# Strassen-Winograd products for gate and up, and a down stage of its own, in a hybrid decoder layer

## The chip, the cores and the metric

The kernel runs on one core of one Trainium2 chip. The metric is the device time of one execution in microseconds. The names of the engines are those of the profile: PE is TensorE (PEld its weight loads), DVE VectorE, ACT ScalarE, POOL GpSimd and SP the queue that issues most DMAs.

## What is computed

One decoder layer over T = 1032 tokens (1024 of a prompt and 8 single new tokens), model width D = 1024, feed-forward width 2816:

```python
h = x + 0.5 * swiglu(rmsnorm(x, g_ff1), w_ff1_gate, w_ff1_up, w_ff1_down)
z = rmsnorm(h, g_mix) @ w_in              # latents of MLA, and q, k, v, o, gates of mLSTM
...                                       # attention (8 heads), mLSTM (4 heads), caches
h = h + concat(rmsnorm(a), headnorm(m)) @ w_out
h = h + 0.5 * swiglu(rmsnorm(h, g_ff2), w_ff2_gate, w_ff2_up, w_ff2_down)
h = h + sigmoid(rmsnorm(h, g_ple) @ w_ple_gate) * (pe @ w_ple_proj)
y = rmsnorm(h, g_final)
# swiglu(x, wg, wu, wd) = (silu(x @ wg) * (x @ wu)) @ wd
```

## The kernel before

Activations lie feature-major: 8 tiles of 128 features by 1032 tokens, and the tokens are worked on in three groups of N = 344. Every large product is done with each operand split in two fp32r parts, hi and lo, and three matmuls, hi·hi, hi·lo and lo·hi (`mm3`, L198 to L200). `split` (L180, L184) makes the parts: ScalarE casts hi, and VectorE (or GpSimd, L182) subtracts it.

`ffn` runs both feed-forward blocks. Its unit is one block of 128 of the 2816 hidden features (there are 22, called f) for one token group: 24 matmuls for gate into the bank pg, 24 for up into pu, then silu, the product with up (L355), and the split into the tiles hd, which stay in SBUF. f is taken in blocks of 5, 5, 5, 5 and 2. After each block `down` multiplies its hidden features with the down weight into pd and adds half of it to h (L367). In the last block units and downs of the groups alternate (`halves`, `close`), so that the next norm can start (`nxt.a` sums squares, `nxt.b` scales and splits).

The first FFN starts on tokens that are not normalised yet (`lift`, L295): its gate and up banks are multiplied by the norm's factor r afterwards (L349, L351). The second one uses `n2`, whose groups are normalised during the output projection.

`ple_proj` computes the projection of the per-layer embedding, 8 row tiles × 3 groups of 6 matmuls (bank pj), stored to the DRAM tensor ppd. It is a generator: `em.add(ple_proj(), PP_E, PP_D)` hands it to the emitter, which puts a unit of it between the instructions of the attention each time a number of estimated microseconds has been spent. The attention's other tiles: pss scores (L1166), pT transposes (L1198), po products with v (L1221), and for the new tokens ss (L1074) and ol, whose cached keys kt and nt GpSimd gathers (L1051, L1060).

TensorE and SP run in the order in which the program issues their instructions; ScalarE, VectorE and GpSimd are ordered by the scheduler.

## Time and profile before

| what | value |
|---|---|
| median of 3 runs | 2342.53 us (2341.18 to 2345.26) |
| the profiled execution, its own time | 2340.3 us |
| its span in the trace | 2338.5 us |
| mean granted clock of TensorE | 0.989 |
| matmuls | 14,543 |
| DMA | 167.28 MB, 72 GB/s on the mean |

The span runs from the first to the last recorded instruction; 1.8 us of the execution lie around it. Busy times of the engines overlap, so they are read against the span one by one. A matmul's recorded duration overlaps its neighbours' too; the distance between starts is what a stream of them costs.

### The profile page before, as it was taken

How to read it: one execution, taken by the hardware profiler on the slowest of the kernel's cores; microseconds unless marked ns; L12 is line 12 of the kernel's file. 1: busy time of each engine (PE TensorE's matmuls, PEld its weight loads, DVE VectorE, ACT ScalarE, POOL GpSimd, SP SyncE). 2: the span in 40 equal slices, each digit the busy share in tenths (PEclk: the TensorE clock that was granted, in tenths of full speed). 3: DMA queues.
4: the chain of work that ended last, by engine and by line, in shares of the span. 5: the costliest groups of instructions: out<-in, count | busy, mean ns of one | idle time of the engine just before them, and what ended most of it. 6: DMA issues, size and time to landing. Idle time of an engine off the chain costs nothing.

```text
span 2338.5 us, 35223 instructions
## 1 busy us (share of the span) xinstructions
PE 2288.4 (98%) x14543; PEld 2178.7 (93%) x14543; DVE 1046.3 (45%) x2147; ACT 708.7 (30%) x1448; POOL 410.4 (18%) x397
## 2 busy tenths in 40 slices
PE   8999999999999899999999999999999999999997
PEld 8999999999999799999756579999999999999996
DVE  7332232332334747446656677423223223223575
ACT  5211211211212433434555553321120210211353
POOL 4100101101102421112376325100000000000243
PEclk9999999999999999999999999999999999999998
DMA  3111112011021322223755531101112112112113
GB/s 136 39 53 55 30 53 64 25 56 55 28 68 55 137 34 94 83 74 127 198 154 150 161 109 37 46 27 56 55 32 73 32 38 72 37 34 81 58 39 107
DMA packets 73752, 167.28 MB, mean 72 GB/s; under 512 B 10656, under 2 KB 36864, under 8 KB 73592
## 3 DMA queue, kind: packets, MB, share of 16 engines
q1 hardware_dynamic: 63304, 142.69, 19.6%
q0 software_dynamic: 6832, 18.12, 3.0%
q10 hardware_dynamic: 3456, 4.23, 0.6%
q8 instruction: 114, 1.87, 0.3%
q14 instruction: 46, 0.38, 0.1%
HBM read 141.33 MB, written 23.65 MB: 71 GB/s over the span
## 4 chain that ended last, share of the span: by engine, by line
PE 89%; DVE 6%; ACT 2%; DMA 1%; issue 1%; POOL 0%; SPq 0%; DVEq 0%; ACTq 0%; POOLq 0%
PE pd L199 7%; PE pd L200 7%; PE pd L198 7%; PE pg L200 7%; PE pu L199 7%; PE pu L198 7%; PE pu L200 7%; PE pg L199 7%; PE pg L198 7%; PE pz L199 3%; PE pz L198 3%; PE pz L200 3%; PE pss L1166 3%; DVE xf L281 2%; PE po L1221 2%; PE pT L1198 2%
## 5 line engine op out<-in xcount | busy, mean ns | idle before, releaser
L198 PE MATMUL pd<-hdh,wh 128*128 128x344 f32 x1056 | 340.6, 323 | 5.9 <-ACT hdh L180 5.9
L199 PE MATMUL pd<-hdl,wh 128*128 128x344 f32 x1056 | 339.6, 322 | 3.4 <-DVE hdl L184 3.3
L199 PE MATMUL pg<-xn,wh 128*128 128x344 f32 x1056 | 338.7, 321 | 2.8 <-DVE xn L184 1.9
L198 PE MATMUL pg<-xn,wh 128*128 128x344 f32 x1056 | 338.3, 320 | 1.7 <-ACT xn L180 1.3
L200 PE MATMUL pd<-hdh,wl 128*128 128x344 f32 x1056 | 339.1, 321 | 0.0
L198 PE MATMUL pu<-xn,wh 128*128 128x344 f32 x1056 | 338.7, 321 | 0.3 <-DVE si L349 0.3
L200 PE MATMUL pg<-xn,wl 128*128 128x344 f32 x1056 | 338.4, 320 | 0.5 <-DVE wl L184 0.4
L199 PE MATMUL pu<-xn,wh 128*128 128x344 f32 x1056 | 338.1, 320 | 0.0
L200 PE MATMUL pu<-xn,wl 128*128 128x344 f32 x1056 | 338.0, 320 | 0.0
L180 ACT CAST wh<-wr 128x1024 fp32r<-128x1024 f32 (+2 forms) x195 | 180.4, 935 | 371.7 <-PE pd L199 304.6
L184 DVE TENSOR_TENSOR wl<-wr,wh 128x1024 fp32r<-128x1024 f32 (+2 forms) x195 | 216.0, 1108 | 115.4 <-ACT wh L180 110.3
L355 DVE TENSOR_TENSOR hp<-si,pu 128x344 f32<-128x344 f32 x132 | 67.6, 512 | 420.6 <-PE pu L200 413.1
L367 DVE SCALAR_TENSOR_TENSOR h<-pd,h 128x344 f32<-128x344 f32 x240 | 122.9, 514 | 281.3 <-PE pd L200 281.3
L256 POOL TENSOR_TENSOR sq<-sq,sq 128x344 f32<-128x344 f32 x66 | 70.0, 1060 | 798.5 <-ACT sq L251 771.2
L198 PEld LDWEIGHTS pd<-hdh,wh 128*128 128x128 f32 x1056 | 199.9, 189 | 7.1 <-ACT hdh L180 6.7
L199 PEld LDWEIGHTS pd<-hdl,wh 128*128 128x128 f32 x1056 | 199.9, 189 | 4.6 <-DVE hdl L184 4.2
L199 PEld LDWEIGHTS pg<-xn,wh 128*128 128x128 f32 x1056 | 199.0, 188 | 4.2 <-DVE xn L184 3.1
L198 PEld LDWEIGHTS pg<-xn,wh 128*128 128x128 f32 x1056 | 199.0, 188 | 2.4 <-ACT xn L180 1.6
L200 PEld LDWEIGHTS pg<-xn,wl 128*128 128x128 f32 x1056 | 199.0, 188 | 1.1 <-DVE wl L184 1.1
L200 PEld LDWEIGHTS pd<-hdh,wl 128*128 128x128 f32 x1056 | 200.0, 189 | 0.0
L198 PEld LDWEIGHTS pu<-xn,wh 128*128 128x128 f32 x1056 | 199.0, 188 | 1.0 <-issue 0.8
L199 PEld LDWEIGHTS pu<-xn,wh 128*128 128x128 f32 x1056 | 199.0, 188 | 0.2
(374 smaller groups left out, 3974.9 us busy)
## 6 DMA issues: line engine op xcount, KB each, us to landing
wr<-in_wu SPq DMA_DIRECT2D x44, 512.0 KB, 3.6
wr<-in_wg SPq DMA_DIRECT2D x43, 512.0 KB, 3.7
wr<-in_wd SPq DMA_DIRECT2D x64, 320.0 KB, 2.9
wr<-in_w_in SPq DMA_DIRECT2D x22, 512.0 KB, 6.2
h<-in_xT SPq DMA_DIRECT2D x24, 172.0 KB, 4.3
hsp<-h SPq DMA_DIRECT2D x8, 516.0 KB, 2.6
ppd<-pj SPq DMA_DIRECT2D x24, 172.0 KB, 3.3
h<-hsp SPq DMA_DIRECT2D x8, 516.0 KB, 3.9
```

The costliest lines, as they stand in the source:

```text
L180: act.copy(hi, src)
L184: dve.tensor_tensor(out=lo, in0=src, in1=hi.bitcast(F32), op=ALU.subtract)
L198: pe.matmul(ps, whi, xhi, start=first, stop=False)
L199: pe.matmul(ps, whi, xlo, start=False, stop=False)
L200: pe.matmul(ps, wlo, xhi, start=False, stop=last)
L256: pool.tensor_tensor(out=acc[0], in0=acc[0], in1=q, op=ALU.add)
L281: dve.scalar_tensor_tensor(out=x, in0=s[:, c], scalar=gc[:, g0 + k:g0 + k + 1], in1=r, op0=ALU.mult, op1=ALU.mult)
L355: dve.tensor_tensor(out=p, in0=s, in1=pu, op=ALU.mult)
L367: dve.scalar_tensor_tensor(out=h[m][:, c], in0=pd, scalar=0.5, in1=h[m][:, c], op0=ALU.mult, op1=ALU.add)
L1166: pe.matmul(ps[:, 0:n], qp[:, qs], kp[0:96, kc], start=True, stop=True)
L1198: pe.transpose(ps[:, PV_POS[j], :], P[j][:, kb * 128:(kb + 1) * 128], ident)
L1221: pe.matmul(po[64 * i:64 * i + 64, p0 * 128:256], v, px[:, 2 * i + p0:2 * i + 2, :].rearrange("p j q -> p (j q)"), start=kb == 0, stop=kb ...
```

## The change

- **Gate and up.** Tokens are cut in quarters of QN = 258; two quarters form a half of HC = 516. For each half and each of gate and up, a pair of f (256 hidden features), the model width's two halves and two quarters of tokens make a 2 × 2 by 2 × 2 block product. It is done with seven block products for eight (Winograd's form). `operands` makes the eight token operands once per FFN: the four blocks b11, b21, b12, b22 of the normalised tokens, and four differences t1 to t4, all split. `weights` loads a pair's 2 × 512 KB and builds the weight operands with four 512-column sums, and splits. `chain(i)` runs the products b11, b21, t2, t1, t3, t4, b22, each 12 matmuls of 258 columns for each half, with copies c1, u2 and u3 out of the banks. The first pair of each FFN is done with all eight products (`plain`).
- **Hidden features.** silu(gate) · up is stored by GpSimd's DMA queue in DRAM (hidd), unsplit.
- **Down** is a stage behind all gate and up products, in five passes: halves mh of the output features and token groups, (0, g0 and g1), (0, g2), (1, g0), (1, g1), (1, g2), each over all 22 f in PSUM. Hidden blocks of three f are read back (hr) and split, the down weight is read in a new layout once per half, and the residual h is read back, from the input or from a spill hsp2.
- **Start.** The embedding's projection runs at the start of the program, in two parts around the sums of squares. The first FFN's tokens are loaded as rows xr and normalised before the products; lift and the later scaling are gone.
- **Second FFN.** Its norm's factors r2 and first operands are built during the output projection (BUILD_AT).

```diff
-FBLOCKS = [5, 5, 5, 5, 2]
+QN = T // 4
...
+AHEAD_D = 5
...
+AH_IN = {(3, 12): (0,), (4, 4): (1,), (4, 12): (2,)}
+PL_A, PL_B = 13, 5
+BUILD_AT = (2, 4, 5, 6)
...
+    def operands(at, rr, g0, hf, x):
...
+        for n, kh, j in (("b11", 0, 0), ("b21", 1, 0), ("b12", 0, 1), ("b22", 1, 1)):
+            q = 2 * hf + j
+            t = raw[n] = B([128, 4, QN], F32, "xf")
+            for k in range(4):
+                kk = 4 * kh + k
+                dve.scalar_tensor_tensor(out=t[:, k, :], in0=at(kk, q), scalar=gc[:, g0 + kk:g0 + kk + 1], in1=rr[:, QS[q]], op0=ALU.mult, op1=ALU.mult)
+            put(n, t)
+            yield
+        t = None
+        for n, a, b in (("t1", "b12", "b11"), ("t3", "b22", "b12"), ("t2", "b22", "b11"), ("t4", "b21", "b22")):
+            o = "b22" if n == "t2" else "b21" if n == "t4" else b
+            dve.tensor_tensor(out=raw[o], in0=raw[a], in1=raw[b], op=ALU.subtract)
+            put(n, raw[o])
...
+    def weights(ap, j, plain):
...
+            put(("b11", "b21"), r1)
+            s1 = B([128, 512], F32, "ws")
+            dve.tensor_tensor(out=s1, in0=a21, in1=a22, op=ALU.add)
+            dve.tensor_tensor(out=a21, in0=a11, in1=a21, op=ALU.subtract)
+            dve.tensor_tensor(out=a11, in0=s1, in1=a11, op=ALU.subtract)
+            dve.tensor_tensor(out=a12, in0=a12, in1=a11, op=ALU.subtract)
+            yield
+            put(("t2", "b22"), r1)
...
+        def store(i, hf, o):
+            pool.dma_start(out=hidd[i - 1:i + 1, :, hf * HC:(hf + 1) * HC].rearrange("a p c -> p a c"),
+                           in_=o.rearrange("p (a q) n -> p a (q n)", a=2))
...
+        def chain(i):
...
+            for hf in product(b1, "b11", True, True):
+                o[hf] = B([128, 4, QN], F32, "hp" if up else "gs")
+                c1[hf] = SC(QN, p="c1")
+                act.copy(c1[hf], b1[hf])
...
+            for hf in product(b2, "b21", True, True):
+                dve.tensor_tensor(out=o[hf][:, 0], in0=b2[hf], in1=c1[hf], op=ALU.add)
...
+            for hf in product(b1, "t2", False, True):
+                u2[hf] = SC(QN, p="u2")
+                act.copy(u2[hf], b1[hf])
...
+            for hf in product(b3, "t1", True, True):
+                pass
+            for hf in product(b1, "t3", False, True):
+                u3[hf] = SC(QN, p="u3")
+                act.copy(u3[hf], b1[hf])
+                dve.tensor_tensor(out=o[hf][:, 3], in0=b3[hf], in1=u3[hf], op=ALU.add)
...
+            for hf in product(b1, "t4", False, True):
+                if up:
+                    dve.tensor_tensor(out=o[hf][:, 2], in0=b1[hf], in1=gs[hf][:, 2], op=ALU.mult)
...
+            for hf in product(b3, "b22", False, True):
+                dve.tensor_tensor(out=o[hf][:, 1], in0=b3[hf], in1=u2[hf], op=ALU.add)
...
+        passes = [(0, (0, 1)), (0, (2,)), (1, (0,)), (1, (1,)), (1, (2,))]
+        seq = [(p, f) for p in range(len(passes)) for f in range(NF)]
...
+        def load_hid(p, g, t):
+            n = min(3, NF - 3 * t)
+            raw = B([128, 3, N], F32, "hr")
+            sp.dma_start(out=raw[:, 0:n], in_=hidd[3 * t:3 * t + n, :, GS[g]].rearrange("f p c -> p f c"))
+            hi, lo = (B([128, 3, N], F32R, x) for x in ("hh", "hl"))
+            split(hi[:, 0:n], lo[:, 0:n], raw[:, 0:n])
...
+        for n, (p, f) in enumerate(seq):
+            mh, gset = passes[p]
+            fetch(n + AHEAD_D)
+            if f == 0:
+                acc = {(m, g): PS([128, N], "pd") for m in range(4) for g in gset}
...
+                    mm3(acc[m, g], whi[:, f % 2, c], wlo[:, f % 2, c], hi[:, f % 3, :], lo[:, f % 3, :], f == 0, f == NF - 1)
+                    if f == NF - 1:
+                        t = h[4 * mh + m][:, GS[g]]
+                        dve.scalar_tensor_tensor(out=t, in0=acc.pop((m, g)), scalar=0.5, in1=t, op0=ALU.mult, op1=ALU.add)
...
+    load_rows(0)
+    pre1 = ({0: weights(I["wg1"], 0, True), 1: weights(I["wu1"], 0, True)}, {}, {})
+    load_rows(1)
+    X1 = [{}, {}]
+    st = [stat1(q) for q in range(2)]
+    for _ in range(PL_A):
+        next(pl, None)
+    for f in st:
+        f()
+    g1 = [operands(row, r1, G_FF1, hf, X1[hf]) for hf in range(2)]
...
-    em.add(ple_proj(), PP_E, PP_D)
```

**TensorE at the start of the program**, after the warming matmuls pw. Before, the first gate products on the lifted tokens xn come at once (wh and wl are the halves of a weight):

```order
L445 MATMUL pw_113<-ones 128x128 [waits DVE_49]
L445 MATMUL pw_113<-ones 128x128 x13
L198 MATMUL pg_289<-xn_92,wh_140 128x344 [waits Activation_49]
L199 MATMUL pg_289<-xn_92,wh_140 128x344 [waits Pool_49]
L200 MATMUL pg_289<-xn_92,wl_141 128x344 [waits DVE_49]
L198 MATMUL pg_289<-xn_92,wh_140 128x344
```

After the change 24 units of pj stand there; this is the last of them and what follows it, two sums of squares ns (of 258 tokens each) and the first plain product cp:

```order
L204 MATMUL pj_479<-peh_106,wj_123 128x344 [waits Activation_49]
L205 MATMUL pj_479<-pel_107,wj_123 128x344
L206 MATMUL pj_479<-peh_106,wj_124 128x344
L204 MATMUL pj_479<-peh_112,wj_123 128x344
L205 MATMUL pj_479<-pel_113,wj_123 128x344
L206 MATMUL pj_479<-peh_112,wj_124 128x344
L271 MATMUL ns_488<-sq_390,ones 128x258 [waits DVE_49,Activation_49]
L271 MATMUL ns_497<-sq_413,ones 128x258 [waits DVE_49,Activation_49]
L418 MATMUL cp_529<-xh_334,wh_512 128x258 [waits Activation_49]
L419 MATMUL cp_529<-xl_335,wh_512 128x258
L420 MATMUL cp_529<-xh_334,wl_513 128x258 [waits DVE_49]
```

The 144 pj products have moved ahead of all gate products, and the first gate product now waits behind two norm sums as well.

**TensorE in the attention.** Before, units of pj stand between transposes and scores:

```order
L1198 MATMUL pT_11705<-ident,P_11515 128x128 x2
L1129 MATMUL pot_11712<-ident,ols_11662 128x128 x2
L198 MATMUL pj_11717<-peh_11072,wj_11540 128x344
L199 MATMUL pj_11717<-pel_11073,wj_11540 128x344
L200 MATMUL pj_11717<-peh_11072,wj_11540 128x344
L198 MATMUL pj_11717<-peh_11078,wj_11540 128x344
L199 MATMUL pj_11717<-pel_11079,wj_11540 128x344
L200 MATMUL pj_11717<-peh_11078,wj_11540 128x344
L1166 MATMUL pss_11729<-kT_10479,qT_11267 128x512
L1166 MATMUL pss_11732<-kT_10479,qT_11267 128x512
```

After the change a comparable place holds the attention's own products alone:

```order
L1439 MATMUL po_12475<-PT_12507,vv_11720 64x128 x2
L1384 MATMUL pss_12560<-kT_11597,qT_12349 128x384
L1439 MATMUL po_12475<-PT_12507,vv_11720 64x128
L1416 MATMUL pT_12572<-ident,P_12353 128x128
L1416 MATMUL pT_12572<-ident,P_12392 128x128
L1416 MATMUL pT_12572<-ident,P_12436 128x128
L1416 MATMUL pT_12572<-ident,P_12483 128x128
L1384 MATMUL pss_12581<-kT_11597,qT_12349 128x512
L1416 MATMUL pT_12589<-ident,P_12353 128x128
```

The pj units are gone from here; the rest of the attention keeps its products.

**SP and VectorE in the last passes of the first FFN's down stage**, after the change; before, hidden features stayed in SBUF and nothing of this existed. On SP (with what each DMA waits for) hr are hidden blocks and wr weights of the next stage:

```order
L533 DMA hr_7367<-hid_511 128x3x344 [waits DMAHW2_49,PE_49]
L533 DMA hr_7440<-hid_511 128x3x344 [waits PE_49]
L533 DMA hr_7529<-hid_511 128x3x344 [waits DMAHW3_49,PE_49]
L199 DMA wr_7547<-in_w_in 128x1024 [waits DMAHW4_49,PE_49]
L533 DMA hr_7577<-hid_511 128x3x344 [waits DMAHW1_49,DMAHW5_49,DVE_49,PE_49]
L533 DMA hr_7619<-hid_511 128x3x344 [waits PE_49]
L199 DMA wr_7661<-in_w_in 128x1024 [waits DVE_49,PE_49]
```

Each load of a hidden block waits for the place of an older one, which TensorE releases with its last product on it: for hr_7529 that is 38 matmuls ahead of the first one that uses it. On VectorE the subtract for that block (hl_7532) stands behind the norm of the group before (r, xf, and u, the operands of the next stage):

```order
L287 SCALAR_TENSOR_TENSOR xf_7485<-h_5920,gc,r_7477 128x344
L287 SCALAR_TENSOR_TENSOR xf_7489<-h_5988,gc,r_7477 128x344
L287 SCALAR_TENSOR_TENSOR xf_7493<-h_6056,gc,r_7477 128x344
L287 SCALAR_TENSOR_TENSOR xf_7497<-h_6112,gc,r_7477 128x344
L287 SCALAR_TENSOR_TENSOR xf_7501<-h_6794,gc,r_7477 128x344
L287 SCALAR_TENSOR_TENSOR xf_7505<-h_6832,gc,r_7477 128x344
L287 SCALAR_TENSOR_TENSOR xf_7509<-h_6870,gc,r_7477 128x344
L287 SCALAR_TENSOR_TENSOR xf_7513<-h_6902,gc,r_7477 128x344
L190 TENSOR_TENSOR u_7473<-xf_7505,u_7473 128x344
L190 TENSOR_TENSOR u_7474<-xf_7509,u_7474 128x344
L190 TENSOR_TENSOR u_7073<-xf_7513,u_7474 128x344
L190 TENSOR_TENSOR hl_7532<-hr_7529,hh_7531 128x1032
```

The norm's steps are in front of the block that TensorE needs next.

## Rows read from the trace of the kernel before

**Rows 1.** Part 1 of the page, the busy time of each engine, its share of the span and the number of its instructions.
```profile
PE 2288.4 (98%) x14543; PEld 2178.7 (93%) x14543; DVE 1046.3 (45%) x2147; ACT 708.7 (30%) x1448; POOL 410.4 (18%) x397
```

**Rows 2.** Part 4 of the page, the chain of work that ended last, by engine.
```profile
PE 89%; DVE 6%; ACT 2%; DMA 1%; issue 1%; POOL 0%; SPq 0%; DVEq 0%; ACTq 0%; POOLq 0%
```

**Rows 3.** Part 5 of the page, groups of TensorE instructions. Columns: line, engine, operation, out and in, shapes, count, busy us and mean ns of one, idle time before and its releaser.
```profile
L198 PE MATMUL pd<-hdh,wh 128*128 128x344 f32 x1056 | 340.6, 323 | 5.9 <-ACT hdh L180 5.9
...
L198 PE MATMUL pg<-xn,wh 128*128 128x344 f32 x1056 | 338.3, 320 | 1.7 <-ACT xn L180 1.3
...
L198 PE MATMUL pu<-xn,wh 128*128 128x344 f32 x1056 | 338.7, 321 | 0.3 <-DVE si L349 0.3
```

**Rows 4.** Windows of 100 us in the first FFN: length, then busy us and (in x) the instructions that start, for PE, PEld, DVE, ACT and POOL, then the granted clock, the DMA share and GB/s.
```profile
100.00:200.00 100.00, 100.00 (x638) 100.00 (x637) 32.78 (x54) 15.10 (x24) 6.07 (x6) 1.00 0.20 59
...
600.00:700.00 100.00, 100.00 (x637) 100.00 (x636) 33.85 (x55) 16.80 (x26) 6.04 (x6) 1.00 0.16 48
```

**Rows 5.** Windows, same columns: the first 100 us, four microseconds of the loading at the start, and ten at the start of the second FFN.
```profile
0.00:100.00 100.00, 92.43 (x540) 88.24 (x541) 61.44 (x102) 45.29 (x87) 34.23 (x36) 0.97 0.28 96
8.00:12.00 4.00, 2.03 (x8) 1.80 (x9) 4.00 (x9) 1.88 (x5) 2.28 (x2) 0.87 1.05 389
1360.00:1370.00 10.00, 6.29 (x28) 2.81 (x28) 7.90 (x11) 6.75 (x14) 4.05 (x3) 0.66 0.71 235
```

**Rows 6.** Windows, same columns: 20 us in the last block of the first FFN and of the second.
```profile
760.00:780.00 20.00, 13.63 (x63) 12.27 (x62) 13.07 (x23) 8.33 (x16) 6.39 (x6) 0.74 0.49 184
2200.00:2220.00 20.00, 17.10 (x99) 16.48 (x97) 18.73 (x30) 11.47 (x23) 10.68 (x9) 0.91 0.31 89
```

**Rows 7.** Timeline of TensorE around products of 512 columns and, between them, of 128 columns in plain fp32. Columns: start us, us, engine, line, operation, out and in, shapes, count.
```profile
1123.42 0.27 PE L695 MATMUL pko<-ident,km 128*128 128x128 f32 x1
1123.53 0.27 PE L696 MATMUL pko<-ident,om 128*128 128x128 f32 x1
...
1124.76 0.39 PE L199 MATMUL ps<-ckl,ukh 128*128 128x512 f32 x1
...
1125.92 0.39 PE L198 MATMUL ps<-ckh,ukh 128*128 128x512 f32 x1
```

**Rows 8.** Timeline of the weight loads after a wait of TensorE (in brackets).
```profile
1073.12 0.19 PEld L198 LDWEIGHTS ps<-cqh,uqh 128*128 128x128 f32 x1 [1.61 <-ACT uqh L180]
1073.23 0.19 PEld L199 LDWEIGHTS ps<-cql,uqh 128*128 128x128 f32 x1
```

**Rows 9.** Groups of ScalarE and VectorE with their shapes apart, columns as in rows 3.
```profile
L180 ACT CAST wh<-wr 128x1024 fp32r<-128x1024 f32 x129 | 132.7, 1044 | 128.8 <-PE pd L199 111.2 <-DMA wr<-in_wu 9.9 <-DMA wr<-in_wd 5.3
...
L1253 ACT COPY pj<-pj 128x344 f32<-128x344 f32 x24 | 10.8, 449 | 3.7 <-PE pj L200 3.5
...
L184 DVE TENSOR_TENSOR wl<-wr,wh 128x1024 fp32r<-128x1024 f32 x129 | 161.0, 1249 | 79.5 <-ACT wh L180 79.3
...
L355 DVE TENSOR_TENSOR hp<-si,pu 128x344 f32<-128x344 f32 x132 | 67.6, 512 | 420.6 <-PE pu L200 413.1 <-POOL si L351 7.5
L281 DVE SCALAR_TENSOR_TENSOR xf<-h,gc,r 128x344 f32<-128x344 f32 x72 | 66.4, 991 | 0.3
```

**Rows 10.** Timeline of TensorE in the attention, a unit of six pj products and what follows it.
```profile
1257.52 0.40 PE L198 MATMUL pj<-peh,wj 128*128 128x344 f32 x1
...
1258.64 0.65 PE L1221 MATMUL po<-PT,vv 128*64 128x256 f32 x4
```

**Rows 11.** Waits of TensorE between 1150 and 1310 us: engine, tile and line, what was waited for, us in total, times, longest us.
```profile
PE ss L1074 <- DMA kt<-in_cT,idx_t: 1.9, 1, 1.9
PE pj L198 <- ACT wj L180: 1.6, 1, 1.6
PE pj L200 <- DVE wj L184: 1.5, 1, 1.5
```

**Rows 12.** Groups of GpSimd with their shapes apart, the gathers.
```profile
L1060 POOL DMA_INDIRECT nt<-in_cN,idx_n x64 | 62.6, 979 | 19.5 <-issue 15.2 <-PE pss L1166 0.9 <-DMA nt<-in_cN,idx_n 0.6
L1051 POOL DMA_INDIRECT kt<-in_cT,idx_t x64 | 60.6, 948 | 57.5 <-DVE dn L822 28.9 <-issue 14.7 <-PE pT L1198 10.2
```

**Rows 13.** Window over the part of the attention with the gathers, columns as in rows 4.
```profile
1150.00:1310.00 160.00, 155.06 (x1077) 92.03 (x1076) 104.07 (x334) 95.23 (x266) 114.33 (x119) 0.98 0.60 164
```

**Rows 14.** Timeline of TensorE at the start of the program.
```profile
6.27 0.42 PE L198 MATMUL pg<-xn,wh 128*128 128x344 f32 x1 [0.37 <-ACT wh L180]
...
10.39 0.42 PE L199 MATMUL pg<-xn,wh 128*128 128x344 f32 x1 [0.77 <-POOL xn L182]
...
11.54 0.49 PE L198 MATMUL pg<-xn,wh 128*128 128x344 f32 x1
11.83 0.49 PE L199 MATMUL pg<-xn,wh 128*128 128x344 f32 x1
...
14.12 0.43 PE L198 MATMUL pg<-xn,wh 128*128 128x344 f32 x1
```

**Rows 15.** DMA issues: out and in, queue, kind, count, KB each, median us from issue to landing.
```profile
wr<-in_wu SPq DMA_DIRECT2D x44, 512.0 KB, 3.6
...
wr<-in_w_in SPq DMA_DIRECT2D x22, 512.0 KB, 6.2
...
h<-hsp SPq DMA_DIRECT2D x8, 516.0 KB, 3.9
...
xr<-xd SPq DMA_DIRECT2D x4, 512.0 KB, 7.0
```

More of the change, by code (lines that the diff above doesn't have):

```diff
@@ L25 @@
 NF = D_FF // 128
-FBLOCKS = [5, 5, 5, 5, 2]
+QN = T // 4
+QS = [slice(q * QN, (q + 1) * QN) for q in range(4)]
+HC = 2 * QN
+NPAIR = NF // 2
+NCH = 2 * NPAIR
+AHEAD_D = 5
 HEADS = 8
@@ L84 @@
 SA_E, SA_D = 4.5, 14.0
-PP_E, PP_D = 3.5, 33.0
 TSIM = True
@@ L244, in rsqrt, with norm_a @@
         return r
-    def norm_a(srcs, c):
+    def norm_a(srcs, c, adds=POOL_ADDS):
         n = c.stop - c.start
@@ L251, in norm_a @@
             act.activation(q, s[:, c], AF.Square)
-            j = 0 if i < POOL_ADDS else 1
+            j = 0 if i < adds else 1
             if acc[j] is None:
@@ L439, in trunk @@
     qzr = C([128, 3 * NB_S * 32], name="qz")
-    def begin(w, hid):
-        act.activation(warm, epsc, RSQ)
-        pw = PS([128, 128], "pw")
-        for i in range(WARM):
-            pe.matmul(pw, ones, ones, start=i == 0, stop=i == WARM - 1)
-        sp.dma_start(out=gc, in_=I["gcols"])
-        load_x(0, 0, 2)
-        for k in range(2):
-            n1.lift(0, k)
-        w0 = [loadw(I["wg1"][0], KD, 2)]
-        load_x(0, 2, KD - 2)
-        for k in range(2, KD):
-            n1.lift(0, k)
-        w0.append(loadw(I["wu1"][0], KD))
-        w[0] = w0
-        hid[0] = pair("hd")
-        load_x(1)
-        for k in range(KD):
-            n1.lift(1, k)
-        n1.a(0)
-        load_x(2)
-        for k in range(KD):
-            n1.lift(2, k)
@@ new lines, in trunk, with load_rows, row @@
+    act.activation(warm, epsc, RSQ)
+    pw = PS([128, 128], "pw")
+    for i in range(WARM):
+        pe.matmul(pw, ones, ones, start=i == 0, stop=i == WARM - 1)
+    pl = ple_proj()
+    next(pl)
+    rows = [None, None]
+    def load_rows(hf):
+        rows[hf] = [B([128, 2, HC], F32, "xr") for _ in range(4)]
+        for i in range(4):
+            sp.dma_start(out=rows[hf][i], in_=I["xT"][256 * i:256 * i + 256, hf * HC:(hf + 1) * HC].rearrange("(k p) c -> p k c", k=2))
+    def row(k, q):
+        return rows[q // 2][k // 2][:, k % 2, (q % 2) * QN:(q % 2 + 1) * QN]
@@ new lines, in trunk, with stat1 @@
+    r1 = B([128, T], F32, "rr")
+    def stat1(q):
+        acc = norm_a([row(k, q) for k in range(KD)], slice(0, QN), 3)
+        return lambda: norm_r(acc, D, QN, r1[:, QS[q]])
+    load_rows(0)
[8 more added lines that the diff above has]
+    g1 = [operands(row, r1, G_FF1, hf, X1[hf]) for hf in range(2)]
@@ L478, in trunk, with build1 @@
+    next(g1[0])
+    next(g1[0])
+    for _ in range(PL_B):
+        next(pl, None)
+    st = [stat1(q) for q in range(2, 4)]
+    for _ in pl:
+        pass
+    for f in st:
+        f()
+    st = f = None
+    done1 = [2]
+    def build1(n):
+        while done1[0] < n:
+            next(g1[done1[0] // 4 % 2])
+            done1[0] += 1
+            if done1[0] == 8:
+                rows[0] = rows[1] = None
     ident = C([128, 128], name="ident")
@@ L1400, in trunk, with build2 @@
     aT = None
-    n2.h = h
     mixin.g[0] = None
-    n2.a(0)
-    em.later(LAT_W, lambda: n2.b(0))
+    X2 = [{}, {}]
+    r2 = B([128, T], F32, "rr")
+    hsp2 = tc.dram_tile([D, T], F32, name="hsp2")
+    stat = {0: norm_a(h, GS[0])}
+    h2 = list(h)
+    g2 = [operands(lambda k, q: h2[k][:, QS[q]], r2, G_FF2, hf, X2[hf]) for hf in range(2)]
+    done2 = [0]
+    def build2(n):
+        while done2[0] < n:
+            next(g2[done2[0] // 4 % 2])
+            done2[0] += 1
+            if done2[0] == 8:
+                h2.clear()
+    em.later(LAT_W, lambda: norm_r(stat.pop(0), D, N, r2[:, GS[0]]))
     for m in range(KD):
@@ L1407, in trunk @@
     mixin.g[1] = None
-    n2.a(1)
-    em.later(LAT_B, lambda: n2.b(1))
+    stat[1] = norm_a(h, GS[1])
+    em.later(LAT_B, lambda: norm_r(stat.pop(1), D, N, r2[:, GS[1]]))
     for m in range(KD):
         out_unit(m, 2)
+        if m in BUILD_AT:
+            build2(1 + BUILD_AT.index(m))
     mixin = None
-    n2.a(2)
-    def begin2(w, hid):
-        for f in range(2):
-            w[f] = [loadw(I[x][f], KD) for x in ("wg2", "wu2")]
-            hid[f] = pair("hd")
-    mid2 = {MID2: lambda _: n2.b(2)}
+    stat[2] = norm_a(h, GS[2])
+    for k in range(KD):
+        pool.dma_start(out=hsp2[k * 128:(k + 1) * 128, :], in_=h[k])
+    h = []
+    pre2 = ({i: weights(I[x], 0, True) for i, x in enumerate(("wg2", "wu2"))}, {}, {})
+    em.later(LAT_B, lambda: norm_r(stat.pop(2), D, N, r2[:, GS[2]]))
     npl = Norm(h, "xp", G_PLE)
```

373 lines of the change are left out of this document (224 added, 149 removed).

## The prediction

> **What bounds the kernel now.** I read the page's busy times first, then the chain, the groups, the windows, and last single stretches of the timeline. TensorE is busy for 98% of the span, VectorE for 45%, ScalarE for 30% [rows 1], and TensorE has 89% of the chain that ended last [rows 2]. So a change is worth what it takes from or adds to TensorE's queue, and the other engines matter where they make it wait. The page lists gate, up and down in kinds of 1056 matmuls [rows 3]: two products with three kinds each are 6 × 1056 = 6336 gate and up matmuls, and down has 3168. The "mean ns" there is not their price, since they overlap. The windows give it: 637 or 638 products start in every 100 us [rows 4], one per **156.9 ns**. In these windows VectorE is busy for about a third and ScalarE for a sixth: the stage is a plain stream of matmuls. What is not stream is short: the first 100 us hold 540 [rows 5], and the ends of the two FFNs fall to 63 and 99 in 20 us [rows 6], where 127.5 would fit.
>
> **Part 1, gate and up.** They go from 6336 products of 344 columns to 7488 of 258: per FFN one f pair of each weight stays plain, with 384 products, and 20 chains have 7 operands × 2 token halves × 12 = 168 each; (384 + 3360) × 2 = 7488. That is 18% more instructions with 11% fewer columns, so everything hangs on one price that no row has: a 258-column product behind its own weight load. Two rows bound it. Products of 512 columns start every 0.232 us, (1125.92 − 1124.76)/5 [rows 7]. Against 156.9 at 344 that is a slope of 75.1/168 = 0.447 ns per column and a fixed part of only 3 ns: by the line 258 columns cost 118.5, in plain proportion 117.7. I take **118.2**, between them. The floor is the weight load: 0.11 us between two loads with nothing else in the way [rows 8], and 128-column products, which have a load each, also start 0.11 us apart [rows 7]. So 258 columns lie just above where columns stop mattering. Sum: 6336 × 156.9 = 994.1 us before, 7488 × 118.2 = 885.1 after, **−109 us**. The ends: 112 gives 838.7 (−155), 125 gives 936 (−58), and 156.9, no gain per column at all, +181.
>
> The Trainium skill ("TensorE: Matmul & The Clock Gate", section "Back-to-back issue gap") prices a single warm product at N/2.4 + 2.5 ns, so 145.8 for 344 columns and 110.0 for 258. The trace has 156.9 for the first and so disagrees; by the rule the sum would be −170 in place of −109.
>
> Can the others feed it? A chain lasts 168 × 118 = 19.8 us. VectorE does in it three 128x1024 subtracts (1.25 us [rows 9]), one of 512 and four 512-column sums (an estimate of 0.70 each from the same row) and the evacuations, about 13 us; ScalarE three casts of 1.04 [rows 9], copies and silu, 6 to 10 us. Operands are ready some 120 products ahead. The tightest wait: t4 accumulates on the bank that ScalarE has copied after t3, one block of 12 products (1.4 us) earlier; a copy of 344 columns takes 0.45 [rows 9] and I count no stall. If a 1.04 us cast stood in front of each, 0.2 us would be lost 40 times, which the bounds hold. Two pairs of weights, 2 MB in two chains of 39.6 us, are 53 GB/s, as now [rows 4], and the gated stores another 27.
>
> **Part 2, attention without the embedding products.** The order shows 24 units of six pj products gone from between the scores. Each held TensorE's path 1.12 us with its exposed load and the turn to the next kind, 1257.52 to 1258.64 [rows 10]; at 6 × 0.157 plus a load, 1.02 each, they are 24.5 us, and their weights made 3.1 us of waits [rows 11]. Not all comes back: GpSimd starts 128 gathers there at 0.95 to 0.98 us each [rows 12], 123 us, and is busy 114 of the 160 us from 1150 to 1310 [rows 13]. With 25 us less it has some 135 us for 114, and the wait of the ss products for kt [rows 11] is next; I give back 7. **−20**, between −10 and −27.
>
> **Part 3, the start.** The same 144 products now stand ahead of the first gate product: 144 × 0.157 = 22.6 us. Before, TensorE began at 6.27 [rows 14] and lost 20 us of the first 100: 540 products, 30 of them not of the stream, leave 510 × 0.157 = 80 us of work [rows 5]. Now two embedding tiles and two weight tiles, 2.1 MB, come first; the DMAs move 389 GB/s there [rows 5], so 5.4 us of transfer and then cast and subtract: first pj at about 10. Token rows, squares, sums and the real norm (before, the first products ran on tokens not yet scaled) are hidden under the pj stream until about 35, the first gate product comes near 40, and in the plain stage VectorE has about 50 us for 16 operand blocks against 45 us of products. I expect 27 lost where it was 20: 22.6 + 7 gives **+30**, between +20 and +42. Each stall may also cost a stretch at the lower clock: after the wait that ended at 10.39 the products start 0.29 us apart until 14.1, the lower level of 1.2 GHz [rows 14].
>
> **Part 4, the down stage.** Its 3168 products keep their 344 columns: no change in the stream. What changes is how blocks arrive. With 22 f in PSUM the old last block of two f goes, with its 63 and 99 products in 20 us: 64.5 × 0.157 = 10 and 28.5 × 0.157 = 4.5 us come back [rows 6]. New: hidden blocks are read back from DRAM by SP's queue, three f each, into two places. In SP's order, shown with the change, the load of hr_7529 waits for TensorE's last use of the block before the previous one, and its first product comes 36 to 38 later, 38 × 0.157 = 6.0 us. The way needs 3.6 to 3.9 us for a transfer of 512 KB [rows 15], 1.05 cast, 1.25 subtract [rows 9] and hand-overs, nearly 7: about 1 us late wherever it is not fetched ahead. In the last pass VectorE's queue has in front of that subtract three norm steps, eight xf and three subtracts, which the order shows; at 0.5 to 0.99 us each [rows 9] about 13 us, so I count 3 us there and 2 in the pass before. Four pass ends with 0.8 each and the clock after the stalls bring 11 per FFN. 22 − 14.5 = **+8**, between −5 and +25. Behind SP's waiting loads stand the next stage's weights (wr from w_in), which come late with them; their first use is after the pass, so I cost that at nothing, and at the stall itself if a pass end finds them missing.
>
> **Part 5, start of the second FFN.** Its first operand blocks are built during the output projection, where before 28 products in 10 us at clock 0.66 showed a stall [rows 5]: **−2**, the spill of the residual lies beside TensorE's work.
>
> Sum: −109 − 20 + 30 + 8 − 2 = −93 on 2340.3, the profiled execution's own time: 2247. The median of the runs shown is 0.1% above that execution, so I say **2249 us**.
>
> **Rivals.**
> *A, the columns run closer to their floor.* If the interval at 258 columns is that of the weight load, 0.11 to 0.112, part 1 gives −155: 2203. For it: load and product overlap. Against it: the rows at 344 and 512 columns lie 9% above one column per cycle of 2.4 GHz, both.
> *B, the round trip through DRAM.* Transfers that meet others take longer: 6.2 us for w_in and 7.0 for xr against 3.6 [rows 15], and a VectorE step at 128x344 took 991 ns where others took 512 [rows 9]. A block late by 4 us in place of 1 at each of 7 loads of two single passes and the ends, in both FFNs, is 40 to 80 us: 2290 to 2330. Against it: DMA carries 40 to 60 GB/s in the FFN windows [rows 4], and the store is 20 us and more ahead of its load.
> *C, slower.* A product has a fixed part that the smaller size repeats 1152 times more. Drawn from 110 ns at 128 columns to 156.9 at 344, a straight line gives 138.2 at 258: 7488 × 138.2 = 1034.9, +41 in place of −109, in all +57: 2399. It decides from 130.6 ns on, (994.1 − 16)/7488. Against it: between 344 and 512 the same construction leaves almost nothing fixed, and the 110 is the load's floor.
> The Trainium skill (same page and section) gives measured sustained spacings of 81 ns at 128 columns and 131 at 512, a large fixed part, which speaks for C. On a line these make 258 columns cost 0.90 of 344; with 156.9 that would be an estimate of 140.8 ns and about 2420 in all. The trace has 0.234 us at 512 and 0.11 at 128, a steeper rise.
>
> **How the numbers follow.** The forecast has 0.71, with a range of its own of 2225 to 2280 (part 1 at 116 to 122, the rest's ends seldom together). A has 0.11, B 0.11, C 0.05, and 0.02 is for a sum of stalls that cancels the gain. A measurement of this kernel tells 0.2%, 4.7 us, from no change. Faster 0.93, same 0.02, slower 0.05. The range goes to A's edge and into B: 2205 to 2300.
>
> **What would show it.** Right: in a window of the chains 845 to 848 products start per 100 us, VectorE is busy near 60% and TensorE 100%; the first cp product near 40 us; the scores follow each other without pj, and the stretch is some 20 us shorter; 11 us lost at the end of each FFN, on hl's subtract or hh's cast. Wrong: fewer than 766 per 100 us in the chains (130.6 ns, rival C), about 900 (A), or windows of the down stage well under 127 products in 20 us (B).

## The result and the profile after

The changed kernel takes **2271.5 us** in the median (2269.9 to 2272.1 in 4 runs), 0.969 of the kernel before with an interval of 0.967 to 0.971: 72 us less, where 93 were forecast. The time lies in the range; the gain is a little over three quarters of what the sum said. Its profiled execution has a span of 2268.1 us, 70.4 less than before. Starts of products on TensorE's timeline cut both spans into the same stages (the first ps here is that of the query latents, ps<-cqh, the row in [rows 8]):

| stage | before | after | difference |
|---|---|---|---|
| start and first FFN, to the first pz | 780.0 | 769.3 | −10.7 |
| input projection, to the first ps | 293.1 | 291.2 | −1.9 |
| attention, to the first wo of group 1 | 332.4 | 316.5 | −15.9 |
| output projection of groups 1 and 2 | 61.7 | 61.7 | 0.0 |
| second FFN, to the first pl | 754.8 | 719.1 | −35.7 |
| embedding's gate and final norm | 116.5 | 110.3 | −6.2 |

Part 1 of the page of after, which answers to [rows 1]: TensorE has 1154 instructions more and is busy 84 us less.

```profile
PE 2204.2 (97%) x15697; PEld 2095.2 (92%) x15697; DVE 1260.9 (56%) x2365; ACT 896.9 (40%) x1736; POOL 351.4 (15%) x363
```

**The price of a product.** Windows of after (length, then busy us and instructions of PE, PEld, DVE, ACT and POOL, the clock, DMA share and GB/s): a long one in the chains, the first 100 us, and two in the last passes of the first down stage. They answer to [rows 4, 5, 6].

```profile
110.00:490.00 380.00, 380.00 (x3164) 380.00 (x3163) 201.90 (x320) 137.64 (x265) 12.86 (x18) 1.00 0.24 81
...
0.00:100.00 100.00, 87.61 (x573) 84.16 (x574) 72.26 (x113) 51.31 (x97) 13.05 (x23) 0.90 0.39 147
...
690.00:700.00 10.00, 8.84 (x46) 8.84 (x47) 3.48 (x3) 1.05 (x1) 0.00 (x0) 0.83 0.15 45
740.00:750.00 10.00, 7.41 (x34) 7.05 (x35) 5.46 (x5) 2.45 (x3) 1.59 (x2) 0.66 0.28 85
```

A long window of before, to measure the old price in the same way:

```profile
100.00:700.00 600.00, 600.00 (x3813) 600.00 (x3812) 191.79 (x312) 104.13 (x167) 51.26 (x50) 1.00 0.16 48
```

A window also counts the two products that began before it and reach into it, so the stream costs 600/3811 = 157.4 ns before (the prediction's 156.9 left that out) and 380/3162 = **120.2 ns** after. TensorE is busy for the whole of the long window, and the page's groups of chain products c show no idle time at all, against 7.7 and 12.7 us ahead of the down products pd:

```profile
L418 PE MATMUL c<-xh,wh 128*128 128x258 f32 x1920 | 543.3, 283 | 0.0
L419 PE MATMUL c<-xl,wh 128*128 128x258 f32 x1920 | 542.3, 282 | 0.0
...
L205 PE MATMUL pd<-hl,wh 128*128 128x344 f32 x1056 | 342.2, 324 | 12.7 <-DVE hl L190 12.7
L204 PE MATMUL pd<-hh,wh 128*128 128x344 f32 x1056 | 342.5, 324 | 7.7 <-ACT hh L186 7.7
```

**The ends of the down stages.** TensorE and VectorE of after, timelines around 690 us, where group 0 has been finished and group 1 runs:

```profile
678.55 0.52 DVE L244 SCALAR_TENSOR_TENSOR r<-t,r 128x344 f32<-128x344 f32 x1
679.11 7.40 DVE L287 SCALAR_TENSOR_TENSOR xf<-h,gc,r 128x344 f32<-128x344 f32 x8
686.42 3.54 DVE L190 TENSOR_TENSOR u<-xf,u 128x344 fp32r<-128x344 f32 x3
689.88 2.36 DVE L190 TENSOR_TENSOR hl<-hr,hh 128x1032 fp32r<-128x1032 f32 x2
```
And TensorE's product that uses it:

```profile
691.16 0.42 PE L205 MATMUL pd<-hl,wh 128*128 128x344 f32 x1 [2.33 <-DVE hl L190]
```

The norm's steps hold VectorE from 679.1 to 689.9; the hidden block's subtract hl stands behind them, and TensorE waits 2.33 us for it. The windows above show what follows: 46 and 34 products in 10 us, at a mean granted clock of 0.83 and 0.66, where 64 would fit. ScalarE is held in the same way: it casts u as each xf arrives, and its cast hh of that block begins at 687.3.

### The profile page after: what moved, and what is told of

It is laid out like the page before. It is cut to its first block, busy times and chain, and to the rows that moved or that the text cites. A ratio compares the mean times of both kernels' runs of the same rounds, so it can differ in the third digit from the quotient of the medians.

```text
span 2268.1 us, 38221 instructions
## 1 busy us (share of the span) xinstructions
PE 2204.2 (97%) x15697; PEld 2095.2 (92%) x15697; DVE 1260.9 (56%) x2365; ACT 896.9 (40%) x1736; POOL 351.4 (15%) x363
## 5 line engine op out<-in xcount | busy, mean ns | idle before, releaser
L418 PE MATMUL c<-xh,wh 128*128 128x258 f32 x1920 | 543.3, 283 | 0.0
L419 PE MATMUL c<-xl,wh 128*128 128x258 f32 x1920 | 542.3, 282 | 0.0
L420 PE MATMUL c<-xh,wl 128*128 128x258 f32 x1920 | 542.1, 282 | 0.0
L419 PEld LDWEIGHTS c<-xl,wh 128*128 128x128 f32 x1920 | 363.7, 189 | 0.0
L420 PEld LDWEIGHTS c<-xh,wl 128*128 128x128 f32 x1920 | 362.6, 189 | 0.0
L418 PEld LDWEIGHTS c<-xh,wh 128*128 128x128 f32 x1920 | 362.4, 189 | 0.0
L205 PE MATMUL pd<-hl,wh 128*128 128x344 f32 x1056 | 342.2, 324 | 12.7 <-DVE hl L190 12.7
L204 PE MATMUL pd<-hh,wh 128*128 128x344 f32 x1056 | 342.5, 324 | 7.7 <-ACT hh L186 7.7
L206 PE MATMUL pd<-hh,wl 128*128 128x344 f32 x1056 | 340.8, 323 | 0.0
L204 PE MATMUL pz<-u,wh 128*128 128x344 f32 x528 | 172.0, 326 | 0.0
L205 PE MATMUL pz<-u,wh 128*128 128x344 f32 x528 | 169.0, 320 | 1.1 <-DVE u L190 0.8
L426 POOL DMA_DIRECT2D hid<-hp x44 | 31.4, 714 | 885.1 <-DVE hp L510 779.8
```

The source lines that it names most:

```text
L204: pe.matmul(ps, whi, xhi, start=first, stop=False)
L205: pe.matmul(ps, whi, xlo, start=False, stop=False)
L206: pe.matmul(ps, wlo, xhi, start=False, stop=last)
L418: pe.matmul(ps, whi[:, c], xhi[:, k, :], start=first and k == 0, stop=False, skip_group_check=True)
L419: pe.matmul(ps, whi[:, c], xlo[:, k, :], start=False, stop=False, skip_group_check=True)
L420: pe.matmul(ps, wlo[:, c], xhi[:, k, :], start=False, stop=last and k == 3, skip_group_check=True)
```

## The experiments

All are timed against the kernel before, run on the same chip beside them, and kernels of different chips are compared by their ratios to it; "after" means the changed kernel and its 2271.5.

**The column price by itself.** Edit, in the kernel before, cut to the loop of one stream (the operands are all ones):

```diff
...
+    def rate(n, step, count=72):
+        ps = PS([128, 512], "sm")[:, 0:n]
+        for i in range(count):
+            k = i // 3 % 4
+            w = sw[i % 3 // 2][:, (k * 128):(k * 128) + 128]
+            x = sx[i % 3 % 2][:, k * step:k * step + n]
+            pe.matmul(ps, w, x, start=i == 0, stop=i == count - 1)
...
```

> The kernel before with 19 streams of 72 products in front of it, each stream with one column count, its own weight load for each product and no waits; only the distance between starts is read, the whole time is not comparable. Theory: the distance goes with the columns above a floor set by the weight load, so 344 gives 157, 258 gives 120 whatever the offset of the moving rows, 256 gives 119, 240 gives 111 to 112 and below that it stays near 110. Rival, alignment: 258 columns at steps of 258 (rows that begin at uneven addresses, as in the changed kernel) give 120, while 258 columns from one fixed address or 256 at steps of 256 give 117 to 118. Second rival, a rounded floor: everything from 192 to 258 columns lies between 110 and 120 on a smooth bend, and 272 and 288 are already on the straight line of 344 and 512.

Windows of 7 us inside the streams of 192, 240, 256, 258 (steps of 258), 258 (one address), 288, 344 and 512 columns:

```profile
32.00:39.00 7.00, 7.00 (x65) 7.00 (x65) 6.64 (x9) 6.29 (x16) 4.69 (x5) 1.00 0.01 4
48.00:55.00 7.00, 7.00 (x65) 7.00 (x65) 0.00 (x0) 0.00 (x0) 0.00 (x0) 1.00 0.01 2
56.50:63.50 7.00, 7.00 (x62) 7.00 (x61) 0.00 (x0) 0.00 (x0) 0.00 (x0) 1.00 0.00 0
65.00:72.00 7.00, 7.00 (x61) 7.00 (x60) 0.00 (x0) 0.00 (x0) 0.00 (x0) 1.00 0.01 2
74.00:81.00 7.00, 7.00 (x61) 7.00 (x60) 0.00 (x0) 0.00 (x0) 0.00 (x0) 1.00 0.00 0
117.00:124.00 7.00, 7.00 (x55) 7.00 (x54) 0.00 (x0) 0.00 (x0) 0.00 (x0) 1.00 0.00 0
138.00:145.00 7.00, 7.00 (x47) 7.00 (x46) 0.00 (x0) 0.00 (x0) 0.00 (x0) 1.00 0.00 0
182.00:189.00 7.00, 7.00 (x31) 5.66 (x31) 0.00 (x0) 0.00 (x0) 0.00 (x0) 1.00 0.00 0
```

First and last start in the streams, over the 71 steps between, give 111 ns at 128, 112 at 192 and 240, 117.8 at 256, 119.8 and 120.0 at 258 (two streams in steps of 258), 130.9 at 288, 156.2 and 157.6 at 344 and 232 at 512. At 258 columns from one address it is 119.4, and at 256 in steps of 258 it is 117.3, so alignment makes half a nanosecond and that rival falls. The bend at the floor is a corner, since 240 still lies on the floor and 256 on the line. The changed kernel stands just above it. Its price of 120.2 is that of the column count; the chains add less than 1 ns to it.

**Eight products in every chain.** The edit takes the differences out and runs the first pair's form everywhere:

```diff
-                wraw[i] = weights(W[i % 2], i // 2, i < 2)
+                wraw[i] = weights(W[i % 2], i // 2, True)
...
-            chain(i)
+            for hf in range(2):
+                for k, _ in enumerate(plain(i, hf)):
+                    if hf == 1:
+                        ready(i + 1, 1)
...
```

> The changed kernel with eight products for seven in every chain: no differences of weights or tokens, all else kept. Theory: the chains are bound by TensorE alone, so the 40 chains' 960 additional products of 258 columns cost 120.1 ns each, +115 us, 2386, and windows of the chains still start 834 per 100 us. Rival: the seven-product chain is held by copies, casts and sums around it, so that the eight plain products cost less than 115 us more; at +60 or less, half of the saving had been given back.

Measured in one run: 2382.6, 111 more than after (112.7 by the spans). Its long window in the first FFN:

```profile
110.00:540.00 430.00, 430.00 (x3582) 430.00 (x3581) 75.18 (x111) 69.38 (x119) 12.84 (x18) 1.00 0.21 71
```

430/3580 = 120.1 ns: the same interval, with VectorE at 17% in place of 53%. The work around the seven products is hidden: the 960 products that were added are worth 115 us, and 111 to 113 came. By the same prices the finer cut alone costs 8448 × 120.1 − 6336 × 157.4 = 17 us; that is a part of the 38 us by which this kernel is slower than the one before, and the rest is what the other parts of the change cost and give back.

**The embedding's projection back in the attention.** Edit: the generator of the kernel before in place of the new one, and, among other lines,

```diff
-    for _ in range(PL_A):
-        next(pl, None)
...
+    em.add(ple_proj(), PP_E, PP_D)
```

> The changed kernel with the embedding's projection back between the attention's products, as the kernel before had it; the first feed-forward block starts without it. Theory: the projection at the start hides part of the loading and of the first norm only: without it the first gate product comes at 18 to 24 us in place of 42, the chains begin about 20 us earlier, and the attention gets its 16 to 18 us back; in all 0 to 8 us less than 2271. Rival: the start is bound by loads and by VectorE's norm and operands anyway, the first gate product stays beyond 32 us and the chains begin less than 12 us earlier; then this kernel is 5 to 17 us slower than 2271.

2270.4 (2267.0 to 2276.2), ratio 0.969 with 0.967 to 0.971: no difference from after that these runs can tell. The chains begin at 84.1 in place of 98.9, and the attention takes 329.6 in place of 316.5; of after's 316.5, 3.2 us are a stretch at the lower clock that this kernel's profiled execution did not have (last section). The last stage takes 113.3 in place of 110.3; the 3 us lie behind the last store of y, and I don't know why. The first gate product comes at 31, not at 18 to 24. The waits of the sums of squares show that TensorE now waits for VectorE's squares at the start:

```profile
11.09 1.23 PE L272 MATMUL ns<-sq,ones 128*128 128x258 f32 x2 [4.26 <-DVE sq L267]
14.77 1.23 PE L272 MATMUL ns<-sq,ones 128*128 128x258 f32 x2 [2.45 <-DVE sq L267]
25.38 1.23 PE L272 MATMUL ns<-sq,ones 128*128 128x258 f32 x2 [9.39 <-DVE sq L267]
30.27 1.23 PE L272 MATMUL ns<-sq,ones 128*128 128x258 f32 x2 [3.66 <-DVE sq L267]
```

So a third of the projection's 22.7 us at the start fills time in which TensorE would have waited for the norm, and the move as a whole is worth nothing here: 15 us paid, 13 got back in the attention and 3 at the end. The rival's 5 to 17 us were not measured, and the theory's gain is not shown.

**The norms late, in the last pass.** The norm of a group becomes a generator, with a step of one xf and its split per f. The cut shows where the steps are issued:

```diff
...
+            if todo and p == 4 and f >= 2 and next(todo[0], todo) is todo:
+                todo.pop(0)
+                if todo:
+                    next(todo[0])
...
-                em.later(lat[g], lambda g=g: nxt.b(g))
+                if g < G - 1:
+                    todo.append(nxt.steps(g))
+                else:
+                    em.later(lat[g], lambda g=g: nxt.b(g))
```

> The changed kernel with the norms of the token groups 0 and 1 moved from the passes right behind them to the last pass of the down stage, one step per f: the operands of the next stage take their places later, so that hidden blocks have them in the passes before. Theory: TensorE's losses at the end of the down stages (17 and 18 us) come from too few places for hidden blocks and from the norm's steps in front of their subtracts; with loads issued 98 or more products ahead, where it was 38, 10 to 13 us come back in each block: 2245 to 2251, and the waits of pd for hh and hl fall from 20 us to under 6. Rival: the round trip through DRAM is slow in itself, transfers land late when others run; then the waits stay above 14 us and the time within 6 us of 2271.

2247.1 (2241.4 to 2249.8), ratio 0.957 with 0.955 to 0.959, inside the theory's range; the waits fall from 20.4 us to 6.8, a little short of the theory:

```profile
PE pd L205 <- DVE hl L190: 5.7, 6, 1.6
...
PE pd L204 <- ACT hh L186: 1.1, 1, 1.1
```

The loss is real and can be had back, and the DRAM round trip is not slow in itself. But this edit changes two things, the places of the hidden blocks and the order on VectorE.

**The norms in steps, in their old passes.** The same edit without `p == 4`: the program takes the places at the start of the pass, as in after.

> The changed kernel with the norms of groups 0 and 1 issued in steps, one per f, in the passes right behind them as before: the norm's subtracts (u, xp) then stand behind the hidden block's subtract on VectorE, while the operands still take their five places at the start of the pass, so that hidden blocks wait for a place 38 to 74 products ahead. Theory, two causes: the places and the norm's order share the loss about equally; 4 to 14 us less than 2271, and 10 to 20 us more than the late norm with its 2247. Rival, places alone: within 4 us of 2271. Second rival, order alone: within 5 us of 2247.

2242.9 (2240.2 to 2247.5), ratio 0.957 with 0.955 to 0.959: as good as the late norms, and the waits of pd fall to 5.8 us. My two-cause theory's range is missed, and the time is that of the second rival, order alone. VectorE's timeline at the stretch shown for after, in this kernel:

```profile
679.48 5.36 DVE L311 SCALAR_TENSOR_TENSOR xf<-h,gc,r 128x344 f32<-128x344 f32 x8
684.76 1.23 DVE L190 TENSOR_TENSOR hl<-hr,hh 128x1032 fp32r<-128x1032 f32 x1
```

The subtract hl begins at 684.8 in place of 689.9. Two things moved it: the three u subtracts (3.54 us) stand behind it, and the eight xf took 5.36 us in place of 7.40. But a third thing changed, which I had meant to hold: SP issues the loads of this stretch at 667.8, 676 and 686, where after has 675.7, 682 and 688. So this kernel alone does not separate the places from the order.

**The norm without GpSimd, order as in after.** The second of these points at GpSimd, which in after does five of the eight subtracts while VectorE computes the xf. The edit leaves the norm in front and moves the five to VectorE:

```diff
...
-            norm_b(self.acc.pop(g), self.h, self.x.outs(g), self.g0, GS[g])
+            norm_b(self.acc.pop(g), self.h, self.x.outs(g), self.g0, GS[g], lo=0 if g < G - 1 else POOL_LO)
...
```

> The changed kernel with the eight subtracts of the norms of groups 0 and 1 all on VectorE, none on GpSimd; the order stays, the norm in front of the hidden block. Theory: the eight xf took 0.92 us each because GpSimd's subtracts ran beside them, 0.53 to 0.6 alone; norm and subtracts then take 8.5 to 9 us in front of the hidden block where it was 11, the two long stalls of each down stage shorten by about 2 us and the clock with them: 4 to 10 us less than 2271. Rival: the xf are slow for another reason, or the five more subtracts eat it: 2269 to 2280.

2248.1 (2246.3 to 2248.6), ratio 0.959 with 0.957 to 0.960: 23 us less than after, where I had expected 4 to 10. VectorE at the same stretch:

```profile
679.39 3.99 DVE L287 SCALAR_TENSOR_TENSOR xf<-h,gc,r 128x344 f32<-128x344 f32 x8
683.29 3.50 DVE L190 TENSOR_TENSOR u<-xf,u 128x344 fp32r<-128x344 f32 x8
686.71 3.10 DVE L190 TENSOR_TENSOR hl<-hr,hh 128x1032 fp32r<-128x1032 f32 x2
```

Eight xf and eight subtracts take 7.5 us where eight xf and three subtracts took 10.9: help from GpSimd made VectorE's part longer. hl begins 3.2 us earlier, TensorE does not wait at this place, and the waits of pd fall to 8.6 us in all. This kernel also settles the places. The first load of the stretch, on SP in after, in the kernel with steps and in this one:

```profile
675.71 0.36 SPq L533 DMA_DIRECT2D hr<-hid  x1
667.75 8.69 SPq L546 DMA_DIRECT2D hr<-hid  x2
675.99 0.36 SPq L533 DMA_DIRECT2D hr<-hid  x1
```

Here the loads are issued as late as in after (the next two at 682 and 688 in both), and the time comes back all the same. In after that first load had some 7 us to spare, an estimate by the median of 4.3 us from issue to landing: the cast of its block began at 687.3 only, behind the norm. So at this stall the places are not the cause; VectorE's norm in front of the block is.

**Steps and no GpSimd.** Edit on the kernel with steps: `split(hi, lo, x)` for all k.

> The changed kernel with the norms of groups 0 and 1 in steps and all their subtracts on VectorE: both edits that took about 25 us each. Theory: they take away the same loss, the wait for the hidden block behind the norm, by its order and by its length, so they do not add: 2236 to 2243, the eight xf again near 4 us and the waits of pd for hh and hl at 4 to 6 us in all. Rival: the order and the contention are separate losses: 2228 or less.

2246.6 (2243.7 to 2248.5), ratio 0.958 with 0.956 to 0.959. They do not add, as the theory says, and the time is even 4 us beyond its end. The eight xf take 4.0 us and the waits of pd are 6.6 us, a little over the 4 to 6 expected.

**The start.** Three edits of the order of loads. In the kernel with late norms the second half of the token rows goes ahead of the first weights:

```diff
+    load_rows(1)
     pre1 = ({0: weights(I["wg1"], 0, True), 1: weights(I["wu1"], 0, True)}, {}, {})
-    load_rows(1)
```

> The kernel with the late norms, with the second half of the token rows loaded ahead of the first gate and up weights. Theory: at the start VectorE is what ends last (it is idle for 17 of the first 30 us and full from 30 on), and the loads of the rows set when it can begin; the second half's rows land some 5 us earlier, the chains begin 2 to 6 us earlier than 99, so 2241 to 2245. Rival: rows are not what it waits for (ScalarE's order, the first factors r): within 2 us of 2247. A mishap that would speak for neither: the first gate product waits for its weights, later than 44 us.

2242.4 (2238.5 to 2244.0), ratio 0.956 with 0.954 to 0.958. The chains begin at 97.7 in place of 99.6, 2 us of the 5, and even these are no sign of the rows: in the kernels whose start is that of after they begin between 97.2 (steps and no GpSimd) and 99.6. The rest lies in the first down stage (253.7 us in place of 258.7). Next, the first half also ahead of the embedding (`next(pl)` behind `load_rows(0)`):

> As the kernel before it in this list, and the first half of the token rows also ahead of the embedding and its weights. Theory: the norm starts some 5 us earlier and the embedding's products, which nobody waits for, 5 us later; the chains begin 6 to 12 us earlier than 99 and the time is 2236 to 2242. Rival: TensorE has to do 69 us of work ahead of the chains and is then the last: its first product at 15 in place of 10 costs the same 5 us, and the time is 2245 to 2252.

2250.6 (2248.6 to 2255.1), ratio 0.960 with 0.958 to 0.961. The first pj comes at 14.8, 5 us later than in its base, the chains begin at 105.5, 8 later, and the kernel is 8 us slower: the rival's time holds, and a later first product is paid in full. Third, the first edit with the projection in the attention again:

> The kernel with late norms and the second half of the rows ahead of the weights, with the embedding's projection back in the attention. Theory: without those products in front, the start is bound by the norm and by VectorE's operands, which the earlier rows speed up: the chains begin near 78, 20 us earlier than 99, the attention gets its 16 us back; 2240 to 2246. Rival: the rows change nothing, so the chains begin at 84 as with the projection alone moved back, 2245 to 2250.

2251.9 (2250.5 to 2253.2), ratio 0.961 with 0.959 to 0.962, outside the theory and a little beyond the rival. The chains begin at 84.1, as without the earlier rows, and the attention takes 333.9. So the order of the second half's loads does not set the start; I have not found what would. Beside its own base, the first edit with 2242.4, this kernel is 9.5 us slower, with intervals that don't touch: the chains begin 13.6 earlier, the attention takes 18.0 more, the last stage 3.1 more and the first down stage 3.8 more. So with the late norms the projection is better placed at the start, where beside after's norms it made no difference. Last, both edits that had looked useful, steps and rows:

> The changed kernel with the norms issued in steps and the second half of the token rows ahead of the first weights, both edits that were measured apart (29 less than 2271 for the first, 5 less than its base for the second). Theory: they act at different places and add: 2237 to 2241. Rival: what the rows gave beside the late norms was mostly a lucky pattern of stalls in the down stage, since the chains began only 1.9 us earlier: 2240 to 2244.

2244.3 (2240.2 to 2248.6), ratio 0.957 with 0.955 to 0.958: the rows add nothing to the steps, and their chains begin at 99.6. What they gave beside the late norms was not theirs. The best of these kernels lie together at 2242 to 2248, with intervals that overlap. The norm without GpSimd is the smallest edit, 23 us less than after, and the norm in steps gives 29; both intervals lie clear of after's (0.957 to 0.960 and 0.955 to 0.959 against 0.967 to 0.971).

## Why the prediction was nearly right, and where it was off

The four groups of terms missed by 12, 4, 3 and 12 us, all to the slow side; only 8 us that the prediction had no term for, in the last stage and the input projection, went the other way.

**Part 1** held in its mechanism: TensorE bound, everything around the products hidden, the price set by the columns. Its size was off: 120.2 in place of 118.2, and 157.4 in place of 156.9, so 900.1 in place of 885.1 and 997.3 in place of 994.1, −97 for −109. In the chains 833 products start per 100 us, where 845 to 848 were said. The line from 344 and 512 columns gave 118.5; the streams by themselves show 1 to 1.5 ns more at 258, 8 ns above the floor. The rivals with the load's price (A) and with a large fixed part (C) are both excluded by that series. The Trainium skill ("TensorE: Matmul & The Clock Gate", section "Back-to-back issue gap") gives 131 ns at 512 columns and 81 at 128 for streams with their own loads; the streams here measure 232 and 111, and the measurement decides.

**Part 2**, −20, measured −15.9. Between the first scores and the first wo 19.1 us are gone, close to the sum. The 3.1 us of waits for wj are replaced by 5.7 of new ones (pnp 2.0, pT 1.9 and 0.5, ol 1.3), of which only ol's 1.3 is a gather's. So the 7 us that I gave back for the gathers came out near by luck. The rest, 3.2 us, went ahead of the first scores, to the clock (below).

**Part 3**, +30, measured +33. The chains begin at 98.9 with 144 × 0.157 + 384 × 0.120 = 68.8 us of work done, so 30 are lost where it was 20 and I had said 27; with the 22.7 of the moved products that is the +33. The clock of these 100 us is 0.90 where it was 0.97 [rows 5]. That pj covers a part of the norm was right, by a third only, as the projection moved back shows.

**Parts 4 and 5** failed in size: +6 together, measured +18. Each down stage lasts 266.4 and 267.5 us for 1584 × 157.4 = 249.3, so 17 and 18 are lost in place of 11. The mechanism was named in the prediction, VectorE's norm in front of the next block, and the kernels with the norm in steps and without GpSimd show that it makes most of the loss: their down stages lose 6 and 5, and 9 and 7 us. Two steps were wrong. I priced the places (38 products ahead) beside it, and the norm without GpSimd gets its blocks as late as after does and the time back. And I mis-sized what follows a stall. Per stage I counted 8.2 us of waits (3, 2 and four pass ends of 0.8), and 10.5 and 9.9 came; but for the clock I counted 2.8, and 6.6 and 8.3 us are lost outside the waits, two thirds of them between products at the lower level of the clock. That xf costs 0.99 us on the mean in such a place stood in [rows 9]; that this is GpSimd's doing, the norm without GpSimd shows.

**Not foreseen**: the last stage is 6.2 us shorter. Its last norm waits 2.3 us for GpSimd where it waited 4.7, and the 1.6 us of waits for its weights are gone. I have not tested why, nor where the other 2 us lie.

Rival B, 40 to 80 us lost in the down stage, was half right in place and wrong in cause: the hidden blocks land in 4.3 us at the median, and with loads issued at the same times a shorter norm on VectorE brings the time back.

## What to carry to other kernels

A product of a stream is priced by two numbers, the interval of the columns and the floor of its weight load: read both before a cut that trades fewer columns for more instructions. Where a matmul waits for one engine's queue, look at what that queue does in front of it, and shorten or reorder that before buying buffers. And work that is given to a slower engine to help is only help if the first engine does not become slower meanwhile.
